# A value pass packed into 37 columns in place of 54

## Chip, cores, metric

One core of a Trainium2 chip runs the whole program. The metric is the device time of one execution in microseconds (us), lower is better. Engines: PE multiplies matrices (PEld loads its weights), DVE and ACT work on vectors, POOL does general work and issues indirect DMAs, SP issues plain DMAs.

## What is computed

A trunk of two layers for 256 tokens of width 1024. In each layer a token mixer with cross-attention to 256 memory tokens is followed by a layer norm, a PEER feed-forward part and a second norm. The change concerns PEER alone, which has 16384 experts per layer; each token picks 16 for each of 8 heads:

```python
def block(xb):                                   # n = 128 tokens
    q = (xb @ w_q).reshape(n, PEER_HEADS, 2, PEER_HALF)
    s = jnp.einsum('nhpc,pkc->nhpk', q, sk)      # two keys, 128 values each
    sv, si = lax.top_k(s, 16)
    cand = sv[:, :, 0, :, None] + sv[:, :, 1, None, :]
    cand_id = si[:, :, 0, :, None] * 128 + si[:, :, 1, None, :]
    fv, fi = lax.top_k(cand.reshape(n, PEER_HEADS, 256), 16)
    eid = cand_id at fi                          # expert numbers
    gw = jax.nn.softmax(fv, axis=-1)
    act = gelu(jnp.einsum('nhkd,nd->nhk', u_tab[eid], xb))
    return jnp.einsum('nhk,nhkd->nd', gw * act, v_tab[eid])
```

The inputs are drawn with large query, key and expert weights, so that the softmax is steep.

## The kernel before

The program is traced once, so that loops in the code are instructions in a row. Every weight block passes through one machine. `plan` (L1330 on) writes a list `items` in the order of use. `load` (L142) brings an item into one of 5 buffers `raw`: a plain item with a DMA on SP (L150), an item that is a number with an indirect gather on POOL (L156), whose row numbers lie in `vrow`. `pump` (L102) splits an item exactly into a high part `wH` (ACT, L122) and a rest `wL` (DVE, L137, or POOL, L132 and L135); each has 3 buffers. `mm3` (L194) makes three products from the parts, L196 to L198.

PEER does not gather experts by token. It computes dense: expert number = first key × 128 + second key, and the 128 experts with one second key form a column, which is one block of 128 × 1024. Coefficients lie in `lo` (tile `wglo`) for the 64 columns with second key under 64 and in `hi` (`wghi`) for the other 64, by expert and token. The scatter (L1236) puts the routing weight, scaled by 32768 and stored as two fp16 numbers, in its place; the Gelu of the expert's product multiplies it (`finish`, `gated`). Most entries stay 0.

The value pass is the loop `for i in range(NC)` in `peer_layer`. Its first 64 steps, the plain columns, take `lo` and the value table in order. The next `COLS` steps, the packed columns, take only those of the 8192 experts of `hi` that have a coefficient other than 0. `coef(i)` splits the coefficients of column i two steps ahead (`cH` on ACT L251, `cL` on DVE L252), `next` pumps the value blocks three ahead, and `products` makes for each half of the tokens (128) and each half of the width one `mm3` of 128x512: 6 products for one token half, 12 for both. After the last columns, which are kept (3 in layer 0, 6 in layer 1), come the norm and the next stage.

The list of used experts is made on the way by the generator `lists`, one piece per column. It marks for each expert of `hi` which token half uses it, and orders them: only the first half, both, only the second. In that order they get consecutive places in the packed columns. So the first half needs columns 0 to `A_END` − 1, the second columns `B_BEG` to `COLS` − 1 (`blocks`, and `column_order`, which mixes columns of one half with those of both). This holds if the counts fit, which three tests find out; `go` is 1 if all hold:

```python
ok[:, 0:1] = sc[:, nj - 1:nj] >= float(P * B_BEG)          # only the first half
ok[:, 1:2] = sc[:, 2 * nj - 1:2 * nj] <= float(P * A_END)  # first half
ok[:, 2:3] = sc[:, 3 * nj - 1:3 * nj] <= float(P * COLS)   # all
ids = ids * ok                                             # 0 if one fails
```

(shortened from L1080 to L1111). With `crow`, made from `ids`, `lists` gathers the coefficients of each packed column from `rows`, a copy of `hi` in DRAM, two columns per step (`FIRST_GATHER`; `wghi<-rows`, POOL L156). Row 0 of `rows` is zero and stands for an empty place. Afterwards the same queue gathers the values by `vrow` (`raw<-in_v_dram,words`).

Then `dense` (L1123 on) reads `go` on PE and SP and tests it (L1127). If it is 0, the branch loads all 64 value blocks of `hi` and their coefficients into the tile `words` (SP, L1131 and L1132) and makes four products for each in full precision (L255, two instructions each); the packed columns then carry zeros and run all the same. All engines pass the branch.

In layer 0, the items of the next layer's cross-attention, four of `memT` (512 wide) and four of `wkv` (1024 wide), are put between the packed columns (the memory parts). Each takes a `raw` buffer, a cast and a subtraction, but no product in the pass.

Of the kernel before, what the change touches and what calls it, by code (L numbers as in the profile page):

```python
# [25 lines left out]
N0 = 64  # L26
# [2 lines left out]
RAW_BUFS, HL_BUFS = 5, 3  # L29
POOL_COLS = 512  # L30
HALF_COLS = 384
COLS, A_END, B_BEG = 54, 40, 13
NC = N0 + COLS
BIG = 127.0 * 128.0
FIRST_GATHER = 2
STEP_US = 2.65
LATE = 3
EXTRA = 3
# [28 lines left out]
class Trunk:  # L67
# [938 lines left out]
    def lists(self, layer, hi):  # L1006
# [109 lines left out]
        order = self.order[layer]  # L1116
        for k in range(0, COLS, FIRST_GATHER):
            for c in order[k:k + FIRST_GATHER]:
                self.gather(hi[:, c, :], self.rows, crow[:, c:c + 1])
# [17 lines left out]
    def peer_layer(self, layer):  # L1137
        nc, tc, A = self.nc, self.tc, self.A
        with ExitStack() as ctx:
# [11 lines left out]
            with ExitStack() as rctx:  # L1151
# [16 lines left out]
                def route():  # L1168
                    for tt in range(2):
                        for q in range(2):  # L1170
                            self.score(qT, sk, ss[tt], tt, q)
                            yield STEP_US
                    self.pool_cols = D
                    for tt in range(2):
                        yield from self.keys16(w, tt, ss[tt], range(4))
                    while not self.asked:
                        yield STEP_US
                    for tt in range(2):
                        for q in range(2, 4):
                            self.score(qT, sk, ss[tt], tt, q)  # L1180
                        yield STEP_US
                    for tt in range(2):
# [9 lines left out]
                    for _ in range(LATE):  # L1192
                        yield STEP_US
                    self.ready()

                def paced():
                    budget = 0.0
                    for c in route():
                        budget -= c
                        while budget <= 0:  # L1200
                            yield
                            budget += STEP_US - (0.2 + (D - self.pool_cols) / 960 if self.pool_cols < D else 0)
                self.asked = False
# [126 lines left out]
    def plan(self):  # L1330
        A = self.A

        def w(name, n, dts=range(DT)):
            for dt in dts:
                self.add(A[name][dt], n)

        def part(name, dst, k, pool=True):
            fl = lambda t: t[:, 2 * k:2 * k + 2, :].rearrange("p a b -> p (a b)")
            to = lambda: (fl(dst()[0]), fl(dst()[1]))
            to.pool = pool  # L1340
            self.add(A[name][k], 512, to)

        def first(name):
            w(name, 1024, range(3))
            for k in range(4):
                part("memT", lambda: self.mem, k)
                w(name, 1024, (3 + k,))
            w(name, 1024, (7,))

        def norm(n, layer):  # L1350
            for k in "gb":
                ap = A[f"{n}_{k}"][layer]
                self.add(bass.AP(tensor=ap.tensor, offset=ap.offset, ap=[[0, P], [1, D]]), D, None, k)

        def tail(layer):
            for i, dt in enumerate((6, 7, 0, 1, 2, 3, 4, 5)):
                self.add(A["w_out"][layer, dt], D, i - 2 if 0 <= i - 2 < EXTRA else None)
            norm("ln1", layer)
            for g in range(2):
                for dt in range(DT):  # L1360
                    self.add(A["w_q"][layer, g, dt], D)
            for i in range(P):
                self.add(A["u"][layer, i], D)
            for i in range(NC):
                e = i - NC + HL_BUFS + EXTRA
                self.add(A["v"][layer, i] if i < N0 else self.order[layer][i - N0], D,
                         e if layer and 0 <= e < EXTRA else None)
                k = (i - N0 - 4) // 6
                if layer == 0 and i > N0 and (i - N0 - 4) % 6 == 0 and 0 <= k < 8:
                    if k < 4:  # L1370
                        part("memT", lambda: self.mem, k, False)
                    else:
                        self.add(A["wkv"][1, k - 4], D, lambda c=k - 4: self.kvw[c])
            norm("ln2", layer)
        for dt in range(DT):
            self.add(A["xT"][dt // 2][:, dt % 2 * T:(dt % 2 + 1) * T], T,
                     lambda dt=dt: (self.xH[:, dt, :], self.xL[:, dt, :]))
            self.add(A["w0kg"][dt], 896, cuts=2 if dt < 2 else 1)
        first("w0qx")
        for c in range(4):  # L1380
            self.add(A["wkv"][0, c], D)
        w("w0v", 768)
        w("w0o", 768)
        tail(0)
        w("w1x", 1024)
        w("w1g", 768)
        tail(1)

    def build(self):
# [85 lines left out]
```

## Time and profile before

| | |
|---|---|
| median of 3 runs | 2051.15 us (2051.14 to 2054.2) |
| profiled execution, its own time | 2052.67 us |
| its span, first to last instruction | 2050.9 us |
| mean granted PE clock | 0.987 |
| PE, DVE, ACT, POOL busy | 95%, 66%, 44%, 34% |
| moved by DMA | 396.69 MB |

The profile is of one execution. A group of instructions is named by line, engine, operation and tiles (out<-in); its columns are busy time and mean time of one, then the engine's idle time just ahead of them and what ended it. A product is pipelined: its time (0.39 us) is longer than the distance to the next one, which is what counts. A DMA's landing time is from issue to the last byte.

### The profile page before, as it was taken

The page shows a single profiled execution, that of the slowest core. Times are in us where ns is not written, and L with a number is a line of the kernel's source. Part 1 is how long each engine was busy: PE and PEld are TensorE (multiplying, and loading weights), DVE is VectorE, ACT ScalarE, POOL GpSimd, SP SyncE. Part 2 cuts the span into 40 slices and gives each one's busy share as a digit, 9 for nine tenths or more (in the row PEclk, how much of TensorE's full clock was granted, in tenths as well). Part 3 has the DMA queues.
Part 4 walks back from the last instruction along what each step waited for, and adds up shares of the span by engine and source line. Part 5 has one row for each costly group of instructions (what it writes and reads, how often), then busy time and mean ns, then how long its engine had stood idle before and what let it go on. Part 6 is the DMA issues. An engine that isn't in the chain of part 4 may idle for free.

```text
span 2050.9 us, 34035 instructions
## 1 busy us (share of the span) xinstructions
PE 1952.3 (95%) x12909; PEld 1670.1 (81%) x12909; DVE 1355.4 (66%) x2779; ACT 907.6 (44%) x1566; POOL 688.8 (34%) x553
## 2 busy tenths in 40 slices
PE   8999999999999998998899999999999768999997
PEld 8999999999987776788799999999878543333586
DVE  5674877799999755777848768999997320000276
ACT  5455455555454445646355555554544220000264
POOL 2026832433310376522368334333103450000263
PEclk9999999999999999999999999999999989999999
DMA  6555566556577688765255665566776994555475
GB/s 229 175 174 189 177 194 196 176 165 200 181 220 243 210 249 231 268 240 167 71 185 180 195 195 176 159 203 187 221 240 177 166 228 165 168 172 172 153 265 174
DMA packets 149289, 396.69 MB, mean 193 GB/s; under 512 B 14589, under 2 KB 58626, under 8 KB 148866
## 3 DMA queue, kind: packets, MB, share of 16 engines
q1 hardware_dynamic: 93464, 303.76, 46.4%
q0 software_dynamic: 20736, 70.79, 12.8%
q10 hardware_dynamic: 34922, 19.93, 3.2%
q8 instruction: 102, 1.67, 0.3%
q14 instruction: 65, 0.53, 0.1%
HBM read 376.59 MB, written 17.83 MB: 192 GB/s over the span
## 4 chain that ended last, share of the span: by engine, by line
PE 54%; issue 17%; DMA 13%; POOL 8%; ACT 3%; DVE 3%; SPq 1%; POOLq 0%; DVEq 0%; ACTq 0%
PE bank L197 15%; PE bank L198 15%; PE bank L196 15%; PE bank L255 8%; POOL wL L132 6%; DMA words<-rows 6%; DMA raw<-in_v_dram,words 3%; DMA raw<-in_v_dram 2%; ACT wH L122 1%; POOL raw L156 1%; DVE wL L137 1%; DMA raw<-in_w0kg_dram 1%; SPq L1131 0%; POOL wghi L156 0%; POOL wL L135 0%
## 5 line engine op out<-in xcount | busy, mean ns | idle before, releaser
L122 ACT CAST wH<-raw 128x1024 fp32r<-128x1024 f32 (+2 forms) x584 | 606.1, 1039 | 1024.6 <-PE bank L198 475.0
L137 DVE TENSOR_TENSOR wL<-raw,wH 128x1024 fp32r<-128x1024 f32 (+3 forms) x387 | 437.1, 1133 | 608.7 <-ACT wH L122 606.0
L196 PE MATMUL bank<-xHL,wH 128*128 128x256 f32 x2536 | 715.0, 282 | 0.6 <-ACT wH L122 0.5
L198 PE MATMUL bank<-xHL,wL 128*128 128x256 f32 x2536 | 702.8, 277 | 5.0 <-DVE wL L137 4.8
L197 PE MATMUL bank<-xHL,wH 128*128 128x256 f32 x2536 | 702.2, 277 | 2.2 <-DVE xHL L252 2.1
L198 PEld LDWEIGHTS bank<-xHL,wL 128*128 128x128 f32 x2536 | 476.4, 188 | 7.0 <-DVE wL L137 6.8
L197 PEld LDWEIGHTS bank<-xHL,wH 128*128 128x128 f32 x2536 | 477.0, 188 | 3.0 <-DVE xHL L252 3.0
L196 PEld LDWEIGHTS bank<-xHL,wH 128*128 128x128 f32 x2536 | 476.6, 188 | 1.3 <-ACT wH L122 1.2
L196 PE MATMUL bank<-wH,cH 128*128 128x512 f32 x827 | 328.9, 398 | 21.0 <-ACT cH L251 14.9
L135 POOL TENSOR_TENSOR wL<-raw,wH 128x1024 fp32r<-128x1024 f32 (+1 forms) x124 | 265.0, 2140 | 222.7 <-ACT wH L122 221.9
L197 PE MATMUL bank<-wL,cH 128*128 128x512 f32 x827 | 328.6, 397 | 11.5 <-DVE wL L137 11.4
L198 PE MATMUL bank<-wH,cL 128*128 128x512 f32 x827 | 326.7, 395 | 0.0
L255 PE MATMUL bank<-words 128*128 128x512 f32 x512 | 233.0, 607 | 33.3 <-DMA words<-rows 33.3
L156 POOL DMA_INDIRECT raw<-in_v_dram,words x108 | 133.8, 1239 | 343.5 <-DVE wL L137 270.0
L255 PEld LDWEIGHTS bank<-words 128*128 128x128 f32 x512 | 94.6, 192 | 171.2 <-issue 96.7
L132 POOL TENSOR_TENSOR wL<-raw,wH 128x386 fp32r<-128x386 f32 x126 | 129.6, 1029 | 279.9 <-DVE wL L130 279.9
L156 POOL DMA_INDIRECT wghi<-rows,words x108 | 114.5, 1060 | 272.6 <-DVE words L1113 226.1
L196 PEld LDWEIGHTS bank<-wH,cH 128*128 128x128 f32 x827 | 157.2, 190 | 59.9 <-ACT cH L251 20.8
L197 PEld LDWEIGHTS bank<-wL,cH 128*128 128x128 f32 x827 | 157.4, 190 | 52.8 <-DVE wL L137 21.1
L198 PEld LDWEIGHTS bank<-wH,cL 128*128 128x128 f32 x827 | 157.6, 191 | 34.4 <-DVE cL L252 0.3
L962 DVE TENSOR_TENSOR oh<-iota,i12T 128x1024 f16<-128x1024 f16 x128 | 130.3, 1018 | 0.0
L130 DVE TENSOR_TENSOR wL<-raw,wH 128x640 fp32r<-128x640 f32 x126 | 103.9, 824 | 7.8 <-ACT wH L122 0.3
(330 smaller groups left out, 1885.1 us busy)
## 6 DMA issues: line engine op xcount, KB each, us to landing
raw<-in_u_dram SPq DMA_DIRECT2D x256, 512.0 KB, 3.5
raw<-in_v_dram SPq DMA_DIRECT2D x128, 512.0 KB, 4.2
words<-in_v_dram SPq DMA_DIRECT2D x64, 512.0 KB, 3.5
raw<-in_w_q_dram SPq DMA_DIRECT2D x32, 512.0 KB, 3.8
rows<-wghi ACTq DMA_DIRECT2D x32, 512.0 KB, 5.0
raw<-in_w_out_dram SPq DMA_DIRECT2D x16, 512.0 KB, 4.0
words<-rows SPq DMA_DIRECT2D x64, 128.0 KB, 3.5
raw<-in_w0qx_dram SPq DMA_DIRECT2D x8, 512.0 KB, 5.0
```

The source lines that it names most:

```text
L122: (nc.vector.tensor_copy if self.cast_dve else nc.scalar.copy)(h[:, c], r[:, c])
L130: nc.vector.tensor_sub(l[:, k:], r[:, k:], h[:, k:].bitcast(F32))
L132: nc.gpsimd.tensor_sub(l[:, :k], r[:, :k], h[:, :k].bitcast(F32))
L135: nc.gpsimd.tensor_sub(l[:, :k], r[:, :k], h[:, :k].bitcast(F32))
L137: nc.vector.tensor_sub(l[:, k:], r[:, k:], h[:, k:].bitcast(F32))
L156: self.nc.gpsimd.indirect_dma_start(out=dst, out_offset=None, in_=table, in_offset=bass.IndirectOffsetOnAxis(ap=rows, axis=0))
L196: mm(out, sH, mH, start=start, stop=False, skip_group_check=True)
L197: mm(out, sH, mL, start=False, stop=False, skip_group_check=True)
L198: mm(out, sL, mH, start=False, stop=stop, skip_group_check=True)
L255: self.nc.tensor.matmul(out, lhsT, rhs, start=start, stop=stop, skip_group_check=True)
L962: nc.vector.tensor_tensor(flat(oh[:, 1:3]), self.iota2.unsqueeze(1).to_broadcast([P, 4, P, 2]), pairs(self.i12T[:, j]), op=ALU.is_equal)
```

## The change

```diff
-COLS, A_END, B_BEG = 54, 40, 13
+COLS, A_END, B_BEG = 37, 23, 11
 NC = N0 + COLS
 BIG = 127.0 * 128.0
 FIRST_GATHER = 2
+MEM_STEP = 4
...
-                k = (i - N0 - 4) // 6
-                if layer == 0 and i > N0 and (i - N0 - 4) % 6 == 0 and 0 <= k < 8:
+                k = (i - N0 - 3) // MEM_STEP
+                if layer == 0 and i > N0 and (i - N0 - 3) % MEM_STEP == 0 and 0 <= k < 8:
```

There are 37 packed columns in each layer in place of 54. Columns 0 to 10 are for the first token half alone (before: 0 to 12), 11 to 22 for both (13 to 39), 23 to 36 for the second alone (40 to 53). The three tests compare with 11, 23 and 37 times 128. The memory parts come after packed columns 3, 7 and so on to 31 (before: 4, 10 and so on to 46). Behind the new line, line numbers are higher by 1.

On POOL the row gathers of layer 0 stand like this before (`wghi` are coefficients, `raw` value blocks; the branch row is the test of `go`):

```order
L156 DMA wghi_4672<-rows_75,words_7907 128x256 x38
L156 DMA raw_9357<-in_v_dram,words_7907 128x1024
L156 DMA wghi_4672<-rows_75,words_7907 128x256 x2
L156 DMA raw_9381<-in_v_dram,words_7907 128x1024
...
L156 DMA raw_9547<-in_v_dram,words_7907 128x1024
L1127 UNCONDITIONAL_BRANCH
...
L156 DMA raw_9571<-in_v_dram,words_7907 128x1024
L156 DMA raw_9983<-in_v_dram,words_7907 128x1024
```

and with the change:

```order
L157 DMA wghi_4672<-rows_75,words_7907 128x256 x37
L1128 UNCONDITIONAL_BRANCH
L157 DMA raw_9356<-in_v_dram,words_7907 128x1024
L157 DMA raw_9774<-in_v_dram,words_7907 128x1024
L157 DMA raw_9796<-in_v_dram,words_7907 128x1024
L157 DMA raw_9818<-in_v_dram,words_7907 128x1024
L157 DMA raw_9862<-in_v_dram,words_7907 128x1024
L522 MEMSET kmT_9871 128x1024
L523 MEMSET vm_9872 128x1024
L157 DMA raw_9906<-in_v_dram,words_7907 128x1024
```

All coefficient gathers and the branch now stand ahead of the first value gather; before, the last 16 were mixed with the value gathers.

On DVE, at the first packed columns of layer 0, before (`cL` 128x128 is a column of one token half, 128x256 of both; `memL` is a memory part):

```order
L252 TENSOR_TENSOR cL_9502<-wghi_4672,cH_9501 128x256
L137 TENSOR_TENSOR wL_9520<-raw_9381,wH_9519 128x1024
L252 TENSOR_TENSOR cL_9526<-wghi_4672,cH_9525 128x128
L137 TENSOR_TENSOR wL_9544<-raw_9405,wH_9543 128x1024
L252 TENSOR_TENSOR cL_9550<-wghi_4672,cH_9549 128x256
L1127 UNCONDITIONAL_BRANCH
L137 TENSOR_TENSOR wL_9568<-raw_9429,wH_9567 128x1024
L252 TENSOR_TENSOR cL_9574<-wghi_4672,cH_9573 128x128
L137 TENSOR_TENSOR wL_9980<-raw_9453,wH_9979 128x1024
L252 TENSOR_TENSOR cL_9986<-wghi_4672,cH_9985 128x256
L137 TENSOR_TENSOR memL_9491<-raw_9477,memH_9490 128x512
```

and with the change:

```order
L253 TENSOR_TENSOR cL_9887<-wghi_4672,cH_9886 128x256
L138 TENSOR_TENSOR wL_9903<-raw_9774,wH_9902 128x1024
L253 TENSOR_TENSOR cL_9909<-wghi_4672,cH_9908 128x128
L138 TENSOR_TENSOR wL_9925<-raw_9796,wH_9924 128x1024
L253 TENSOR_TENSOR cL_9931<-wghi_4672,cH_9930 128x128
L138 TENSOR_TENSOR wL_9947<-raw_9818,wH_9946 128x1024
L253 TENSOR_TENSOR cL_9953<-wghi_4672,cH_9952 128x256
L138 TENSOR_TENSOR memL_9876<-raw_9840,memH_9875 128x512
```

Columns of one half and of both alternated; now two or three of one half follow each other, and the first memory part comes one column earlier. The branch has moved seven plain columns ahead of them.

## Prediction

> **What bounds the kernel now.** The page first: its span and its slices of busy tenths for PE and DVE.
>
> ```profile
> span 2050.9 us, 34035 instructions
> ...
> PE   8999999999999998998899999999999768999997
> ...
> DVE  5674877799999755777848768999997320000276
> ```
>
> PE is busy nearly everywhere, so time is won by removing PE work or PE waits. Slices 34 to 37 have a busy PE and an idle DVE, which no other part has. The program's name for what runs there is the tile `words`; its view:
>
> ```profile
> L255 PE MATMUL bank<-words x512: 591/592/1222, 1662.4 to 1928.1; 128*128 128x512 f32 x171
> ...
> L156 POOL DMA_INDIRECT wghi<-rows,words x108: 943/949/1948, 697.8 to 1678.8; - x108
> ...
> L1131 SPq DMA_DIRECT2D words<-in_v_dram x64: 327/328/1084, 1640.1 to 1921.0; - x64
> ```
>
> The 64 loads of line 1131 are one pass through the branch of `dense`, and all lie in layer 1. So layer 1's flag `go` was 0 and the 54 packed columns did not hold its experts; layer 0's flag was 1. I then cut the two value passes into stretches (columns: bounds, length, then busy time and count of PE, PEld, DVE, ACT, POOL, the granted clock, DMA share, GB/s).
>
> ```profile
> 583.71:764.53 180.82, 178.74 (x836) 146.71 (x835) 145.11 (x211) 87.04 (x129) 52.91 (x54) 1.00 0.75 237
> 764.53:901.02 136.49, 121.42 (x489) 92.58 (x488) 87.75 (x121) 75.64 (x116) 73.00 (x62) 0.96 0.79 247
> 1453.58:1659.66 206.08, 188.74 (x837) 149.36 (x836) 144.52 (x210) 86.93 (x129) 51.99 (x54) 0.98 0.80 210
> ...
> 1662.38:1928.17 265.79, 232.47 (x513) 94.44 (x512) 2.98 (x4) 2.60 (x4) 13.15 (x13) 0.97 0.58 170
> 1928.17:2043.25 115.08, 112.01 (x494) 90.69 (x492) 80.13 (x114) 67.45 (x103) 61.95 (x49) 0.99 0.62 219
> ...
> 1935.00:2015.00 80.00, 80.00 (x355) 66.26 (x354) 59.40 (x83) 53.01 (x83) 53.86 (x41) 1.00 0.74 262
> 800.00:890.00 90.00, 84.71 (x357) 65.74 (x356) 65.25 (x87) 56.26 (x86) 47.80 (x39) 1.00 0.79 272
> ```
>
> In order: layer 0's 64 plain columns, its packed columns; layer 1's plain columns, the branch, its packed columns (one more ran at 1659.66, 2.7 us); two stretches inside the packed parts. Layer 1's plain columns do the same work as layer 0's and take 25.3 us longer. A full PE does 355 products in 80 us, 0.225 us each.
>
> **The branch: which test failed, and will it fail again?** The old tests are: only the first token half needs at least 13 columns, the first half at most 40, all at most 54. I counted the reference's own routing (experts with second key from 64, in columns of 128; only first, first half, all). Every chosen expert counted: layer 0 14.6, 38.6, 52.4; layer 1 14.2, 37.3, 51.2. Both would pass, against the rows. But the weight times 32768 is kept in fp16, where anything below 2^-25 becomes 0, and the softmax is steep. Without those: layer 0 13.8, 21.6, 34.6; layer 1 12.7, 20.0, 33.5. Now layer 0 passes and layer 1 fails on 12.7 under 13, as the rows say. If the Gelu zeroes some more, all counts fall; layer 0's first must stay at 13 or above, and there layer 1's is about 12.0. The new limits are 11, 23, 37: both layers pass, by at least 1.0, 1.4 and 2.4 columns. So the branch goes: −265.8 us.
>
> **The slow plain columns of layer 1.** With `go` 0 every index is 0, so all gathers of line 156 read one row. Landing times, layer 0 from 697 to 750, then layer 1 from 1590 to 1640:
>
> ```profile
> raw<-in_v_dram SPq DMA_DIRECT2D x18, 512.0 KB, 4.1
> wghi<-rows,words POOLq DMA_INDIRECT x38, 4.7
> ```
> ```profile
> raw<-in_v_dram SPq DMA_DIRECT2D x10, 512.0 KB, 24.7
> wghi<-rows,words POOLq DMA_INDIRECT x23, 14.7
> ```
>
> Same instructions, 14.7 us for 4.7, and the loads beside them 24.7 for 4.1. With distinct rows I take layer 0's stretch for layer 1: −25.3 us.
>
> **The packed columns.** A column read by one half costs 6 products, by both 12. Before, 27 + 2×27 = 81 blocks, 486 products, 109 us; now 25 + 2×12 = 49, 294 products, 66.2 us; 43 us of PE go per layer. PE takes them only as fast as its supply comes, and columns now average 7.9 products (1.79 us) instead of 9 (2.03 us). The supply, by groups from 800 to 890 us, with the median landing of those gathers:
>
> ```profile
> L137 DVE TENSOR_TENSOR wL<-raw,wH 128x1024 fp32r<-128x1024 f32 x41 | 49.9, 1222 | 25.4 <-ACT wH L122 25.3
> L156 POOL DMA_INDIRECT raw<-in_v_dram,words x39 | 48.0, 1231 | 37.9 <-DVE cL L252 16.5 <-DVE wL L137 12.3 <-issue 4.6
> ...
> L122 ACT CAST wH<-raw 128x1024 fp32r<-128x1024 f32 x41 | 43.1, 1051 | 32.8 <-DMA raw<-in_v_dram,words 21.4 <-PE bank L198 6.1 <-DVE cL L252 2.9
> ...
> L252 DVE TENSOR_TENSOR cL<-wghi,cH 128x128 fp32r<-128x128 f32 (+1 forms) x40 | 13.8, 346 | 0.0
> ...
> L137 DVE TENSOR_TENSOR kL<-raw,kH 128x1024 fp32r<-128x1024 f32 x4 | 5.0, 1260 | 0.0
> L122 ACT CAST kH<-raw 128x1024 fp32r<-128x1024 f32 x4 | 4.2, 1043 | 0.0
> L137 DVE TENSOR_TENSOR memL<-raw,memH 128x512 fp32r<-128x512 f32 x2 | 1.4, 688 | 0.1
> ```
> ```profile
> raw<-in_v_dram,words POOLq DMA_INDIRECT x39, 6.1
> ```
>
> It is a ring: a gather waits for one of 5 `raw` buffers, which DVE frees (releasers L252, L137), then ACT waits for the gather. One turn is 0.3 of issue + 6.1 + 1.05 + 1.22 = 8.7 us; over 5 buffers 1.73 us an item. Measured, with PE a bound for part of the stretch, 41 + 4 + 2 items in 90 us, 1.91. I take 1.8, since PE's share of that bound goes. [...]
>
> Layer 0 has 37 columns and 8 memory parts, the latter now after every 4th column instead of every 6th, each taking a turn: 45 items. When PE reaches the first, 8 are under way (5 raw, 3 split); 37 turns remain, 66.6 us. The tail from the last gather's issue, and the branch test's stall:
>
> ```profile
> 697.83 1.15 POOL L156 DMA_INDIRECT wghi<-rows,words  x1 [113.03 <-DVE words L1113]
> 750.38 1.16 POOL L156 DMA_INDIRECT raw<-in_v_dram,words  x1 [0.30 <-DMA raw<-in_v_dram]
> 770.36 0.97 POOL L521 MEMSET kmT<- 128x1024 f32 x1
> 884.40 1.03 POOL L156 DMA_INDIRECT raw<-in_v_dram,words  x1 [0.30 <-issue]
> 2019.27 0.94 POOL L156 DMA_INDIRECT raw<-in_v_dram,words  x1 [0.30 <-issue]
> ```
> ```profile
> 769.63 0.47 PE L196 MATMUL bank<-wH,cH 128*128 128x512 f32 x1 [2.22 <-PEq L1127]
> ...
> 772.30 0.63 PE L198 MATMUL bank<-wH,cL 128*128 128x512 f32 x1
> 772.73 0.63 PE L196 MATMUL bank<-wH,cH 128*128 128x512 f32 x1
> ```
>
> Tail: 884.40 to 901.02, 16.6 us. The test now stands ahead of plain column 57, so seven plain columns queue behind it on PE, but it costs the same: 2.2 us, and about eight products at 0.43 us (772.30 to 772.73) in place of 0.225, 3.9 us together. Layer 0: 66.6 + 16.6 + 3.9 = 87.1 for 136.5, −49.4 us. Layer 1 has no parts: 37 − 8 = 29 turns, 52.2, plus 2019.27 to 2043.25, 24.0, plus 3.9: 80.1 for 115.1 + 2.7, −37.7 us.
>
> **Small and free edits.** Line 1091's 64 products per layer shrink from 108 to 74 columns: 34/512 × 0.225 × 64 = 1.0 us each layer, −1.9. POOL has 37 row gathers instead of 54; now none stands between the value gathers, which before were issued every third (before: 697.83 to 750.38 for 38, 1.38 us each; after: done at about 749). They still start in time: 749 is 15 us ahead of PE's 764.53. POOL's two fills, 0.97 us each, move behind the fifth value gather; that lead hides them, else they cost 1.9. SP's queue has its own test:
>
> ```profile
> SPq L1127 <- SPq L1127: 3.3, 1, 3.3
> ```
>
> All 64 plain loads stand before it; the first memory part, which stood before it too, now stands behind. It is 3.3 us late at most and has three columns (5 us) ahead of it; uncovered, 3.3. DVE in layer 0's packed part needs 37 × (1.22 + 0.35) + 4 × 1.26 + 4 × 0.69 = 66 us, hidden by the ring's 45 × 1.8 = 81; without that cover it would bind like PE's 66. The last memory part follows column 31, so all are there before their use after column 36.
>
> **Sum.** 49.4 + 25.3 + 265.8 + 37.7 + 1.9 = 380.1; the span falls from 2050.9 to 1670.8. The profiled execution took 2052.67, 1.77 around its span; the median is 1.5 below it. Forecast 1671.
>
> **The rivals.**
> *PE keeps up with the supply.* If transfers land faster than 6.1 us, PE bounds both layers: 66.2 + 3.9 = 70.1 each, gains 66.4 and 47.7; 407 in all, 1644; with a few us of last waits 1650. Layer 1's full stretch of 80 us speaks for it, ACT's 21.4 us of waits for gathers against.
> *The clock falls in the hungry columns.* Layer 1 shows it:
>
> ```profile
> 1609.58 0.50 PE L196 MATMUL bank<-wH,cH 128*128 128x512 f32 x1 [1.47 <-ACT cH L251]
> ...
> 1612.41 0.63 PE L198 MATMUL bank<-wH,cL 128*128 128x512 f32 x1
> ...
> 1610.00:1620.00 10.00, 7.79 (x24) 5.30 (x23) 2.38 (x4) 1.78 (x3) 6.04 (x6) 0.83 0.94 158
> ```
>
> A gap of 1.47 us was followed by products at half pace and 0.83 mean clock. That hides behind the supply except in the tails (3 and 6 columns, 36 and 72 products): at half pace +8 and +16 us at most; I put this at 1685. [...]
> *Layer 0 or 1 still takes the branch.* If one list overflows: +265.8 + 25.3 × 37/54 = 283: 1954.
> *Slower: both take it.* One mechanism: the tables are cut below what the lists hold. It decides when the first half needs over 2944 experts (23 × 128) or all over 4736 in both layers. Then 1671 + 566 = 2237. My count stands 1.4 and 2.4 columns off; a count with every chosen expert would be far over, but the branch rows exclude it.
>
> **How the numbers follow.** Forecast 0.74, clock 0.11, PE-bound 0.08, one branch 0.04, two 0.03. Ring at 1.73 gives gains 4.6 more (2.6 + 2.0), at 1.91 7.3 less (4.1 + 3.2): 1666 to 1678; the range reaches to the two near rivals, 1650 to 1690. A measurement tells 0.2% (4 us). Faster 0.97, same 0, slower 0.03.
>
> **What would show it.** Right: no product of line 255's kind (now 256) anywhere; layer 1's plain columns near 181 us with row gathers landing near 5 us; packed stretches of about 83 and 76 us with ACT waiting for gathers, PE under nine tenths. Wrong: 256-line products in either layer (the count), packed stretches near 67 us with no gather waits (the ring), or a clock near 0.8 in the last columns.

## The result, and the profile after

| | before | after |
|---|---|---|
| median, same chip | 2052.13 us (4 runs, 2051.14 to 2054.2) | 1683.09 us (4 runs, 1681.01 to 1688.04) |
| ratio, 95% interval | | 0.8204 [0.8184, 0.8224] |
| profiled execution, span | 2052.67, 2050.9 us | 1682.1, 1680.3 us |

The change takes 369 us off, 18%. The forecast was 1671 (1650 to 1690), 12 us too low. The page of after, span and busy slices:

```profile
span 1680.3 us, 31641 instructions
...
PE   9999999999999999999798899999999999999896
...
DVE  5675586949999999757668846697699999996476
```

The four slices with a busy PE and an idle DVE are gone. The view of the tile `words` has no product of line 256 and no load of line 1132:

```profile
L157 POOL DMA_INDIRECT wghi<-rows,words x74: 942/1104/1994, 693.2 to 1566.1; - x74
L157 POOL DMA_INDIRECT raw<-in_v_dram,words x74: 935/945/1989, 744.6 to 1647.5; - x74
```

37 gathers of each kind per layer, and no branch in either. The stretches, cut as in the prediction: plain and packed columns of layer 0, of layer 1; then one steady piece of each packed part (columns as there: length, PE, PEld, DVE, ACT, POOL, clock, DMA share, GB/s).

```profile
580.29:762.30 182.01, 178.05 (x837) 145.80 (x835) 142.90 (x211) 87.06 (x129) 47.34 (x49) 1.00 0.74 235
762.30:850.99 88.69, 74.30 (x295) 53.74 (x294) 61.86 (x87) 51.83 (x81) 39.48 (x33) 1.00 0.75 255
1404.12:1591.03 186.91, 180.67 (x836) 147.71 (x835) 143.86 (x211) 87.05 (x129) 46.34 (x48) 0.98 0.73 230
1591.03:1672.70 81.67, 74.95 (x313) 56.86 (x311) 57.51 (x84) 47.26 (x73) 44.34 (x35) 0.96 0.66 223
775.00:835.00 60.00, 49.52 (x192) 34.86 (x192) 42.12 (x59) 36.56 (x58) 30.93 (x26) 1.00 0.80 271
1600.00:1645.00 45.00, 43.04 (x181) 33.04 (x180) 34.80 (x50) 30.70 (x49) 33.17 (x25) 1.00 0.86 290
```

Where the 370.6 us of span went: layer 0's value pass took 317.3 and takes 270.7 (46.6 less); layer 1's, with the branch, took 589.7 (1453.58 to 2043.25) and takes 268.6 (321.1 less). The pass of layer 0 begins 3.4 us earlier (580.29 against 583.71), in code that the change doesn't touch; between and behind the passes 0.5 us are lost.

Layer 1's landing times from 1510 to 1565, where the row gathers of line 157 run:

```profile
raw<-in_v_dram SPq DMA_DIRECT2D x20, 512.0 KB, 4.7
wghi<-rows,words POOLq DMA_INDIRECT x36, 5.0
```

The row gathers land in 5.0 us (14.7 before), the plain loads beside them in 4.7 (24.7). The packed part of layer 0 by groups, 775 to 835 us, and the median landing of its gathers:

```profile
L157 POOL DMA_INDIRECT raw<-in_v_dram,words x26 | 32.1, 1236 | 29.4 <-DVE cL L253 18.4 <-DVE wL L138 8.5 <-issue 1.2
L138 DVE TENSOR_TENSOR wL<-raw,wH 128x1024 fp32r<-128x1024 f32 x26 | 31.8, 1227 | 18.8 <-ACT wH L123 18.6
L123 ACT CAST wH<-raw 128x1024 fp32r<-128x1024 f32 x26 | 27.1, 1048 | 23.4 <-DMA raw<-in_v_dram,words 21.8 <-PE bank L199 1.6
```
```profile
raw<-in_v_dram,words POOLq DMA_INDIRECT x26, 6.0
```

It is the ring again: POOL waits for a buffer that DVE frees, ACT for the gather (21.8 us), DVE for ACT. PE is busy 49.5 of the 60 us. In layer 1's steady piece the ring is less plain: there PE is busy 43.0 of 45 us, so the sign "PE under nine tenths" held in layer 0 only. And the way past the branch on PE's sequencer (L1128; shortest, median and longest time in ns, then first and last start), then the products behind it in each layer:

```profile
L1128 PEldq COMPARE_BRANCH  x2: 5532/6760/7987, 737.5 to 1561.2; - x2
```
```profile
743.15 0.47 PE L197 MATMUL bank<-wH,cH 128*128 128x512 f32 x1 [2.07 <-PEq L1128]
743.46 0.39 PE L198 MATMUL bank<-wL,cH 128*128 128x512 f32 x1
```
```profile
1569.31 0.77 PE L197 MATMUL bank<-wH,cH 128*128 128x512 f32 x1 [4.35 <-PEq L1128]
...
1574.14 0.63 PE L199 MATMUL bank<-wH,cL 128*128 128x512 f32 x1
1574.56 0.53 PE L197 MATMUL bank<-wH,cH 128*128 128x512 f32 x1
```

In layer 0 PE's branch took 5.5 us; PE still had products to work on for all but 2.07 of it, and no product behind it was slow. In layer 1 it took 8.0 us, 4.35 were idle, and twelve products at 0.43 us followed, 2.4 us more.

### The profile page after: what moved, and what is told of

Its sections match the earlier page's. It is cut to its first block, busy times and chain, and to the rows that moved or that the text cites. A ratio compares the mean times of both kernels' runs of the same rounds, so it can differ in the third digit from the quotient of the medians.

```text
span 1680.3 us, 31641 instructions
## 1 busy us (share of the span) xinstructions
PE 1622.9 (97%) x12013; PEld 1498.2 (89%) x12013; DVE 1298.8 (77%) x2711; ACT 861.4 (51%) x1498; POOL 611.3 (36%) x485
## 5 line engine op out<-in xcount | busy, mean ns | idle before, releaser
L123 ACT CAST wH<-raw 128x1024 fp32r<-128x1024 f32 (+3 forms) x550 | 569.9, 1038 | 706.2 <-PE bank L199 213.6
L138 DVE TENSOR_TENSOR wL<-raw,wH 128x1024 fp32r<-128x1024 f32 (+3 forms) x353 | 396.5, 1127 | 296.8 <-ACT wH L123 292.8
L197 PE MATMUL bank<-wH,cH 128*128 128x512 f32 (+1 forms) x699 | 276.2, 395 | 13.2 <-ACT cH L252 6.7
L198 PE MATMUL bank<-wL,cH 128*128 128x512 f32 (+1 forms) x699 | 276.3, 395 | 12.1 <-DVE wL L138 11.9
L199 PE MATMUL bank<-wH,cL 128*128 128x512 f32 (+1 forms) x699 | 274.3, 392 | 0.0
L197 PEld LDWEIGHTS bank<-wH,cH 128*128 128x128 f32 x699 | 132.1, 189 | 43.5 <-ACT cH L252 12.8
L157 POOL DMA_INDIRECT wghi<-rows,words x74 | 79.1, 1068 | 245.6 <-DVE words L1114 223.7
L199 PEld LDWEIGHTS bank<-wH,cL 128*128 128x128 f32 x699 | 132.0, 189 | 28.2 <-DVE cL L253 0.2
L157 POOL DMA_INDIRECT raw<-in_v_dram,words x74 | 91.6, 1238 | 80.5 <-DVE cL L253 41.7
L966 DVE TENSOR_TENSOR oh<-oh,gT 128x1024 f16<-128x1024 f16 x128 | 90.0, 703 | 4.4
L1237 PE MATMUL bank<-oh 128*128 128x128 f16 x1024 | 80.6, 219 | 1.1 <-DVE oh L966 1.1
```

The source lines that it names most:

```text
L123: (nc.vector.tensor_copy if self.cast_dve else nc.scalar.copy)(h[:, c], r[:, c])
L138: nc.vector.tensor_sub(l[:, k:], r[:, k:], h[:, k:].bitcast(F32))
L157: self.nc.gpsimd.indirect_dma_start(out=dst, out_offset=None, in_=table, in_offset=bass.IndirectOffsetOnAxis(ap=rows, axis=0))
L197: mm(out, sH, mH, start=start, stop=False, skip_group_check=True)
L198: mm(out, sH, mL, start=False, stop=False, skip_group_check=True)
L199: mm(out, sL, mH, start=False, stop=stop, skip_group_check=True)
```

## Experiments

The theory to be tested: layer 1 took the branch for the first of the three tests alone; its slow plain columns came from gathers that all read one row; the packed columns are paced by the ring of 5 buffers and its gathers. The rivals: another test failed, so that it was the narrower packing that mattered to the branch; the slow plain columns belong to layer 1 in some other way; PE, the bytes, or POOL's issue sets the pace.

The runs fell on several chips, which differ (before: 2052 us on the chip of the result, 2060 with the first four runs, 2086 and 2081 with two later groups). Times are compared within a group, or as a ratio to before in the same group. Where neither a range nor an interval stands beside a time, the kernel ran once.

### Only the first limit, in the kernel before

```diff
-COLS, A_END, B_BEG = 54, 40, 13
+COLS, A_END, B_BEG = 54, 40, 11
```

> The kernel before with one number changed: the second token half may begin at column 11 in place of 13; still 54 columns, 40 for the first half, memory parts as before. Theory (in layer 1 only the test on the experts of the first half alone failed, 12.7 columns under 13): the branch in layer 1 is gone (-265.8 us) and so are the slow plain columns (-25.3); two more columns are for both halves, 12 products of 0.225 us more per layer (+5.4): 1765 us, no L255 products, plain columns of layer 1 near 182 us. Rival (one of the other two tests failed, so that the gain came from the count of columns): the branch stays, 2051 to 2056 us.

Measured 1778.24 us, before there 2060.32 (0.863). Layer 1's plain and packed columns:

```profile
1455.53:1636.40 180.87, 178.79 (x836) 146.70 (x835) 145.02 (x211) 87.04 (x129) 52.93 (x54) 1.00 0.76 236
1636.40:1768.53 132.13, 120.67 (x517) 96.87 (x515) 83.45 (x118) 70.31 (x107) 78.34 (x64) 0.95 0.72 225
```

No branch, and the plain columns at 180.9 where before had 206.1: the 25.3 us of the prediction to a tenth (layer 0 of this run: 180.8). So one number out of three brings 282 of the 369 us, and the first test alone had failed. One thing was not foreseen: without the branch the 54 packed columns take 132.1 us, not 115.1 + 2.7, which is 14.3 us more. Two more columns for both halves are 2.7 us of that, 12 products at 0.225. PE is also idle for 8.4 us more: 11.5 us of the 132.1, against 3.1 of the 115.1. The test here stands at the first packed columns, where the branch on PE took 5.9 us from 1635.5 us on; in the kernel before, the 31.8 us behind the branch have PE busy throughout. The mean clock is 0.95 against 0.99. What the other 3 us are is not shown.

### The first limit put back, in the changed kernel

```diff
-COLS, A_END, B_BEG = 37, 23, 11
+COLS, A_END, B_BEG = 37, 23, 13
```

> The changed kernel with the second half beginning at column 13 again: 37 columns, 23 for the first half. Theory: layer 1 fails on the first test once more (12.7 under 13) and takes the branch, layer 0 (13.8) does not: 1683 + 265.8 + 17 for the one-row gathers - 5 for two columns of one half in place of both, about 1961 us. Rival: no branch in either layer, 1678 us; or both layers take it, about 2240 us.

Measured 1968.69 us, in the same group. The view of `words`:

```profile
L256 PE MATMUL bank<-words x512: 592/592/1193, 1605.6 to 1858.0; 128*128 128x512 f32 x171
```

The branch is back, in layer 1 alone: one pass of 512 instructions, 253 us. Layer 0 fills at least 13 columns with experts of the first half only, layer 1 fewer than 13. Layer 0 of this run, with the test and with row gathers of spread rows, is the measure for two runs of the same group below; its plain columns:

```profile
581.58:765.30 183.72, 179.66 (x837) 146.94 (x835) 142.88 (x211) 87.04 (x129) 47.32 (x49) 0.99 0.75 233
```

### Limits drawn closer: 35, 22, 12

```diff
-COLS, A_END, B_BEG = 37, 23, 11
+COLS, A_END, B_BEG = 35, 22, 12
```

> The changed kernel with limits just outside the counts: 35 columns, 22 for the first half, the second from 12 (counted: layer 0 34.6, 21.6, 13.8; layer 1 33.5, 20.0, 12.7). Theory (the counts are right): no branch; 45 blocks in place of 49, 5.4 us of PE work per layer, but the supply sets the pace: two turns of 1.9 us fewer per layer, -7.6: 0.816 of before, 7 to 8 us under the changed kernel. Rival (the counts are off by more than half a column): one layer takes the branch, +280 us. Second rival (PE sets the pace): -11 us.

Measured 1979.2 us (1972.69 to 1993.66), ratio 0.9493 [0.944, 0.9547]. The view of `words`:

```profile
L256 PE MATMUL bank<-words x512: 592/592/1193, 1618.4 to 1871.2; 128*128 128x512 f32 x171
```

A miss: the branch in layer 1. With 12 it fails and with 11 it holds, if it is the first test that failed here; the prediction's count for layer 1 was 12.7, and 12.0 if the Gelu zeroes more. So fewer experts are in use there than were counted. The margin of the change itself is therefore under one column in layer 1 (128 experts), not "at least 1.0".

### Limits from the corrected counts: 33, 20, 11

```diff
-COLS, A_END, B_BEG = 37, 23, 11
+COLS, A_END, B_BEG = 33, 20, 11
```

> 33 packed columns, the first half of the tokens in 20, the second in 22 (limits 33, 20, 11). Corrected theory of the counts: layer 1's first-only experts fill between 11 and 12 columns (the run with limits 35, 22, 12 branched in layer 1, the one with 11 did not), layer 0's between 13 and 13.3; of the cut-offs of small weights that give both, every one leaves the first half at most 19.8 columns and all at most 32.6, so no test fails and no branch runs. Ring theory: four columns fewer at 1.9 us in each layer, 15 us less than the control, 0.813 of the time before; packed parts 81 and 74 us. Rival, PE sets the pace: 7 blocks of 6 products at 0.225 us fewer in each layer, 19 us less. Rival, the counts are off again: the branch in one layer, 270 to 285 us more.

The changed kernel went along unchanged, as a control:

> The changed kernel again, as a control on the same chip as the next two. Expected 0.820 of the time before (1683 us where the kernel before takes 2052).

Measured, in the group with before at 2081.18: control 1719.93 us, 0.8262 [0.8238, 0.8286]; 33 columns 1704.45, 0.8187 [0.8167, 0.8208]. No branch. That settles that it was the first test which failed with 35, 22, 12: with 33 and 20 the other two limits are lower still, and they hold. It also shows the prediction's counts for these two too high: all experts in use fit 33 columns in both layers (counted 34.6 and 33.5), and layer 0's of the first half fit 20 (counted 21.6). So the margins of the change there are wider than was said, and that of the first test is narrower; which small coefficients become 0 was not measured. Control, then 33 columns, packed parts of layers 0 and 1:

```profile
786.00:871.10 85.10, 74.50 (x296) 53.68 (x295) 61.83 (x87) 52.20 (x82) 39.73 (x33) 1.00 0.80 266
...
1629.25:1710.80 81.55, 74.05 (x313) 56.23 (x311) 57.13 (x84) 47.09 (x73) 43.62 (x35) 0.98 0.66 225
```
```profile
783.97:862.60 78.63, 65.57 (x254) 46.80 (x253) 56.10 (x79) 46.99 (x74) 36.77 (x30) 0.98 0.79 262
...
1618.22:1694.60 76.38, 67.46 (x271) 49.01 (x269) 51.62 (x77) 41.84 (x65) 37.69 (x31) 0.93 0.63 211
```

The 15.5 us less are what was expected, but the packed parts give 6.5 + 5.2 = 11.7 of them and not 15: layer 1's ran at a clock of 0.93. The rest lies in the plain columns (2.6 and 0.3 less) and between the passes, and isn't explained.

### The changed kernel without the test

```diff
-        self.dense(layer, go, words[:, 512:], self.y)
```

It leaves out the branch for lists that overflow, which these inputs do not take.

> The changed kernel without the branch and its test (the way out for lists that do not fit is left out). Theory: the test costs its PE gaps, 2.07 us in layer 0 and 4.35 in layer 1, and about 2.5 us of half-pace products behind the second: 9 us, 1674 us; layer 1's plain columns fall from 187 to about 180 us. Rival: value gathers are held anyway and another wait takes its place, 1681 to 1684 us.

Measured 1674.16 us (1673.97 to 1674.19), 0.8124 [0.811, 0.8138]. All four stretches:

```profile
581.56:761.23 179.67, 177.78 (x836) 145.85 (x835) 142.88 (x211) 87.05 (x129) 47.33 (x49) 1.00 0.76 238
761.23:848.90 87.67, 75.13 (x296) 55.17 (x295) 61.49 (x87) 51.81 (x82) 41.45 (x33) 0.98 0.79 259
1403.59:1583.28 179.69, 177.81 (x837) 145.85 (x835) 143.35 (x211) 87.05 (x129) 46.29 (x48) 1.00 0.77 239
1583.28:1664.80 81.52, 75.24 (x313) 57.19 (x311) 57.23 (x84) 47.01 (x73) 41.64 (x35) 0.96 0.66 224
```

Plain columns of 179.7 us in both layers, against 182.0 and 186.9 with the test: by that it costs 2.3 and 7.2 us, and layer 1's plain columns are otherwise just like layer 0's. The packed parts change by 1.0 and 0.2, so they do not hold the test's cost. The two kernels ran on different chips; the ratios differ by 0.0080, 16 us, more than these 9.5. On this run's chip layer 0 with limit 13 put back has 183.7, so there the test costs 4.0 us.

### All row gathers read one row

```diff
-        nc.vector.tensor_copy(crow, ids)
+        nc.vector.tensor_scalar(crow, ids, 0.0, None, op0=ALU.mult)
```

`crow` is 0 throughout, `vrow` and `go` are as before; the packed columns get coefficients of zero.

> The changed kernel, with all gathers of coefficients reading row 0 in both layers (the packed coefficients are left out, zeros take their place); no branch is taken. Theory (one row for all is what made the gathers slow): row gathers land in about 15 us in place of 5, and the plain columns of both layers grow by 25.3 x 37/54 = 17 us: 1717 us. Rival (layer 1's slow columns before had another cause, such as the clock or the coming branch): gathers land near 5 us, 1683 us.

Measured 1735.64 us. The plain columns, then the landing times from 700 to 770 us, then the branch on PE:

```profile
582.67:791.85 209.18, 188.54 (x837) 150.00 (x835) 142.93 (x211) 87.00 (x129) 45.08 (x49) 0.95 0.78 204
...
1433.85:1645.08 211.23, 188.90 (x837) 150.28 (x836) 143.26 (x211) 86.98 (x129) 45.16 (x48) 0.94 0.79 203
```
```profile
raw<-in_v_dram SPq DMA_DIRECT2D x16, 512.0 KB, 21.4
wghi<-rows,words POOLq DMA_INDIRECT x35, 15.4
```
```profile
L1128 PEldq COMPARE_BRANCH  x2: 11272/12170/13067, 759.0 to 1610.3; - x2
```
With nothing changed but which rows are read, both layers get the slow gathers (15.4 us, plain loads 21.4) and slow plain columns: 25.5 us more in layer 0 than with limit 13 put back, in the same group, and 27 and 24 over the changed kernel's on the other chip. That is the second theory shown, and it holds for layer 0 as for layer 1. It is more than the 17 us expected; the branch on PE, which now takes 11.3 and 13.1 us in place of 5.5 and 8.0, makes up part of that.

One thing limits the finding. With `go` 0 the value gathers of the kernel before have one index for all rows too (`vrow` is made from `ids`). In its layer 1, from 1935 to 2015 us, 41 of them landed in 5.8 us, no later than layer 0's 6.1 from spread rows. So it is the row gathers, 128 KB from `rows`, that one row makes slow, and not the value gathers, 512 KB from the value table. Why they differ is open.

### What sets the pace of the packed columns

Three kernels on one chip (before there 2086.16 us). The changed kernel as the control:

> The changed kernel itself, beside the next three on one chip: 1683 us, or 0.820 of the kernel before.

The packed value blocks by plain loads of SP, from layer 0's table in order (not the values of the used experts, but the same bytes and the same buffers):

```diff
-                self.gather(r, self.A["v"].rearrange("l i p d -> (l i p) d"), self.vrow[:, ap:ap + 1])
+                self.nc.sync.dma_start(r, self.A["v"][0, N0 + ap])
```

> The changed kernel with the packed value blocks loaded by plain DMAs on SP, block by block of layer 0's table (the values are not those of the used experts). Same bytes, same 5 buffers. Theory (ring): plain loads landed in 4.1 us, so a turn is 0.1 + 4.1 + 1.05 + 1.22 = 6.5 us, 1.3 an item; packed columns about 75 us in each layer, 17 us less. Rival (bytes): 1.87 us an item as before, no change.

And seven buffers in place of five for the value gathers, two of them in space that is free from plain column 62 on:

```diff
+MORE = 2
...
-        while self.n_load < upto and self.n_flight < RAW_BUFS:
+        while self.n_load < upto and self.n_flight < RAW_BUFS + self.more:
...
-            r = self.raw.tile([P, D], F32, name="raw")[:, :n]
+            self.turn += type(ap) is int
+            own = type(ap) is int and self.more and self.turn % (RAW_BUFS + self.more) < self.more
+            r = (self.raw2 if own else self.raw).tile([P, D], F32, name="raw")[:, :n]
...
+                if i + 2 == N0:
+                    self.raw2 = right.enter_context(tc.tile_pool(name=f"raw2_{layer}", bufs=MORE, side="right"))
+                    self.more = MORE
```

> The changed kernel with two more buffers for value gathers, from column 62 on, in the space that the plain coefficients leave. Theory (the ring of 5 buffers sets the pace of the packed columns): a turn of 8.7 us over 7 buffers is 1.24 us an item, so PE (66 us) or DVE (66 us) becomes the bound, packed columns take about 75 us in each layer in place of 88.7 and 81.7: 18 to 20 us less, 0.811 of before. Rival (bytes set the pace, 512 KB at 280 GB/s are 1.87 us): landing grows from 6 to about 8 us, the time stays within 3 us of the changed kernel. Second rival (DVE's chain sets it): no gain in layer 0, some in layer 1.

Measured: control 1726.78 us (1717.29 to 1730.27), 0.8259 [0.8223, 0.8295]; plain loads 1696.87; seven buffers 1714.76 (1703.41 to 1728.66), 0.8224 [0.8165, 0.8283]. The times alone don't tell the seven buffers from five; the stages do. Packed parts of the control, of seven buffers (with a steady piece of layer 1), and of plain loads (the same):

```profile
788.33:875.30 86.97, 74.05 (x296) 53.83 (x295) 61.85 (x87) 52.14 (x82) 41.01 (x33) 1.00 0.79 261
...
1638.36:1720.00 81.64, 75.56 (x313) 56.48 (x311) 57.66 (x84) 47.17 (x73) 40.79 (x35) 0.96 0.66 224
```
```profile
789.72:871.30 81.58, 73.01 (x296) 55.20 (x295) 61.35 (x87) 51.89 (x82) 39.23 (x33) 0.98 0.78 278
...
1628.60:1702.60 74.00, 70.53 (x313) 55.55 (x311) 56.72 (x84) 46.73 (x73) 41.00 (x35) 1.00 0.71 247
...
1636.00:1678.00 42.00, 41.26 (x180) 33.18 (x179) 34.70 (x51) 31.22 (x51) 32.41 (x27) 1.00 0.93 322
```
```profile
785.69:858.80 73.11, 70.82 (x296) 54.24 (x295) 61.61 (x87) 52.83 (x82) 0.00 (x0) 1.00 0.89 306
...
1614.51:1686.70 72.19, 69.70 (x313) 55.83 (x311) 56.45 (x85) 46.98 (x73) 3.27 (x4) 1.00 0.72 248
...
1630.00:1670.00 40.00, 38.90 (x167) 30.86 (x166) 34.93 (x51) 31.74 (x51) 0.00 (x0) 1.00 0.94 325
```

Two more buffers take 5.4 and 7.6 us off the packed parts, so the ring does set the pace; in layer 1 the mean clock rose with it, from 0.96 to 1.00. It is less than the 18 to 20 us expected: layer 0's part was to come to 75 us and takes 81.6. DVE's chain as the bound is out, by which layer 0 would have gained nothing. In layer 1 it is then no longer the ring. POOL's gathers by group and by waits, 1636 to 1678 us, seven buffers:

```profile
L161 POOL DMA_INDIRECT raw<-in_v_dram,words x27 | 32.9, 1218 | 9.6 <-issue 7.9 <-DVE cL L257 1.7
```

POOL waits 1.7 us for buffers in 42 and issues the rest of the time, 1.22 + 0.3 for a gather, 42 us / 27 = 1.56 each; PE is busy 41.3 of the 42, so the two are full together. With plain loads the same bytes come at 325 GB/s and PE is full (38.9 of 40): bytes do not bind at the changed kernel's 223 to 255. The plain loads take 13.9 and 9.5 us off, where PE as the bound was to give 17.0 and 10.0 (83.2 and 76.2 to 66.2).

### Both: 33 columns and seven buffers

The edits of the two sections above together.

> 33 columns (20 and 22) and the two further buffers for value gathers from plain column 62 on. If the two gains are separate: 5.4 and 7.6 us for the buffers (measured with 37 columns) and four columns at 1.56 us in each layer, 25 us less than the control, 0.808 of the time before. If POOL's issue already binds with seven buffers the columns' part stays 12 us; if PE binds the columns' part is 19 us and the buffers bring nothing more. Branch in a layer: 270 to 285 us more.

Measured 1691.94 us (1683.75 to 1694.83), 0.8126 [0.8095, 0.8158], where the control has 0.8262 and 33 columns alone 0.8187:

```profile
785.76:858.00 72.24, 63.21 (x254) 47.34 (x253) 55.56 (x79) 46.65 (x74) 39.01 (x30) 0.98 0.83 286
...
1612.77:1680.50 67.73, 62.63 (x271) 48.96 (x269) 50.82 (x77) 41.58 (x65) 34.67 (x31) 0.97 0.68 239
```

It is 28 us under the control (25 expected), and the packed parts are 12.9 and 13.8 us shorter: the gains add up. This version beats both kernels.

### A trace of before on another chip

On the two chips with before at 2081 to 2086 us the changed kernel's plain columns took 203 to 210 us, not 182 to 187. In layer 0's plain columns of the control of the ring's group PE's longest gap is 6.70 us, in the middle of the row gathers:

```profile
735.08 0.79 PE L197 MATMUL bank<-wH,cH 128*128 128x512 f32 x1 [6.70 <-ACT wH L123]
```

> The kernel before, unchanged, for a trace of it on whichever chip this is. Two chips gave before 2081 to 2086 us and the changed kernel's plain columns 203 to 210 us in place of 182 to 187. If this chip is such a one (time over 2070 us) and the slow plain columns belong to the chip, before's plain columns of layer 0 take over 195 us too (180.8 in the first trace); if they come from the changed order of the gathers, they stay within 5 us of 181. If the chip is like the first one (about 2052 us), the run tells nothing of this.

Measured 2057.7 us, a chip like the first: plain columns of layer 0 180.8 us. It tells nothing of the others. Whether before is slow there in the same columns stays open; the ratios there, 0.826, are a little above the 0.820 of the result.

## Why the prediction was right, and where it was off

**Branch and slow plain columns: right.** The failing test, the layer, the 25.3 us and their cause are each shown (limits 54, 40, 11; limit 13 put back; one row for all). That gives 282 of the 369 us. All gathers of line 156 did read one row, as the prediction says, but that slowed the row gathers and not the value gathers (5.8 us). "Both layers pass, by at least 1.0, 1.4 and 2.4 columns" was too sure for the first: the true margin in layer 1 is under one column, while the counts behind the other two limits were too high. That a weight below 2^-25 becomes 0 was an assumption of the count; no run shows where the cut-off lies. The rival of one branch, at 0.04, was nearer than it looked: a first limit of 12 for 11 meets it.

**The ring: right in kind, its size 5.5 us short in each layer.** Without the test's share the packed parts were forecast at 83.2 and 76.2 us and took 88.7 and 81.7. The last value gathers were issued here:

```profile
835.60 1.03 POOL L157 DMA_INDIRECT raw<-in_v_dram,words  x1 [0.30 <-issue]
```
```profile
1647.50 1.16 POOL L157 DMA_INDIRECT raw<-in_v_dram,words  x1 [0.31 <-issue]
```

PE's first packed products are at 762.30 and 1591.03 us, so that is 73.3 and 56.5 us. The step that failed is "8 are under way": 6 were in each layer (five value gathers and a memory part in layer 0, six gathers in layer 1), so 39 and 31 turns remained, not 37 and 29; at 1.8 us that is 3.6 of the 5.5 us in each. The seventh item, a gather, followed 0.30 and 0.06 us later; whoever counts it as under way has one turn missing, 1.8 us, and the rest of the 5.5 in a slower pace. The late test is not the cause: without it, 6 are under way too. The plain columns' own turns, one gather for one column that PE finishes, stand at 2.7 us just ahead, so the ring is perhaps not yet as full as its buffers allow; that is argued, not shown:

```profile
1585.65 0.94 POOL L157 DMA_INDIRECT raw<-in_v_dram,words  x1 [0.92 <-DVE wL L138]
1588.37 0.94 POOL L157 DMA_INDIRECT raw<-in_v_dram,words  x1 [1.78 <-DVE wL L138]
```

The turns themselves came at 1.88 and 1.82 us with 6 under way, 1.92 and 1.88 with 7, against the 1.8 that was taken and its 1.73 to 1.91. The tails, 15.4 and 25.2 us for 16.6 and 24.0, cancel.

**The test: put at the wrong place, and one price for two.** It was to cost "the same" as before, 3.9 us in each layer, and this was added to the packed parts. It falls in the plain columns and costs 2.3 and 7.2 (4.0 in layer 0 on the other chip). Before, PE met it after the first 38 row gathers; now it stands among the row gathers in both layers, and in layer 1 the branch took 8.0 us. Together 1.7 us over the forecast. The prediction counted PE's gap (2.2 us) and not the branch's own duration (5.7 us in layer 0 of before).

**The sum.** Layer 0 gained 46.6 for 50.4 with its share of line 1091's products, layer 1 321.1 for 329.8, the start 3.4 for nothing, 0.5 lost between: 370.6 for 380.1. The misses are 11 of ring, 1.7 of test and the 0.5, less the 3.4 of start, 9.8 us where 9.5 are missing.

**The rivals.** PE-bound: refuted, since gathers still land in 6.0 us (775 to 835 us) and PE waits; but with plain loads it is nearly true, and with seven buffers in layer 1 too, where POOL's issue is full as well. The clock: in kind there, in size not. Before the last columns of layer 1 stands a gap of 1.70 us, and ten products at 0.43 us or more follow:

```profile
1654.54 0.79 PE L197 MATMUL bank<-wH,cH 128*128 128x512 f32 x1 [1.70 <-ACT cH L252]
...
1656.51 0.63 PE L197 MATMUL bank<-wH,cH 128*128 128x512 f32 x1
```

From 1660 us on the pace is full again; the ten took 5.5 us where 0.225 each makes 2.3, so some 3 us are lost where the rival had up to 16. The time came out at the rival's 1685 all the same, for another reason. In this the range was lucky: by the ring alone the forecast was 1666 to 1678, which 1683 is outside of, and its upper end stood at 1690 for the clock. The gap of 1.70 us, behind several of 0.2 to 0.7, was followed by slow products and the gap of 2.07 us in layer 0 by none, so here the length of the gap alone did not decide.

## To carry to other kernels

Where a fast path has a test and a slow way out, look first which way each layer takes, and try the failing limit alone: here one number gave three quarters of the gain. A data-dependent limit that is tightened needs its margin measured by a run on each side, not counted from a model of the arithmetic. The ring of five buffers was put at turn time over buffers, 1.73 us an item, and came at 1.82 to 1.92; two more buffers, made from space that had become free, took 5.4 and 7.6 us off the packed parts, until another engine was full (POOL's issue and PE, both in layer 1).

## What the runs showed of the hardware

- **Jumping over the branch's code on PE took 3.7 to 13.1 us.** The compare and branch of PE's sequencer took 0.08 and 0.19 us in two of before's three and 5.7 in the third, the jump of layer 0 among its row gathers. Where it jumped with the last row gather issued 17 us or more ahead, it took 3.7 to 4.0 us (33 columns, and the changed kernel itself on the two chips where PE comes to it later); among row gathers 5.5 and 8.0 in the changed kernel, 6.7 and 5.9 in the kernel before with limit 11; beside one-row gathers 11.3 and 13.1. So in these runs it was longer beside gathers; why is not shown.
- **Row gathers whose indices are all equal took three times as long, and slowed the loads beside them.** They landed in 15.4 us, against 4.8 in the changed kernel, where the rows are spread (128 KB each, from `rows`), and the plain loads beside them in 21.4 against 4.8. The 512 KB value gathers of one row were not slow: 5.8 us.
- **The chips differed in one stage.** The same kernel's plain columns took 182 and 187 us on one chip and 203 to 210 on two others, with all other stages within 4 us. PE's long gaps there lie at the row gathers: in the control of the ring's group 17.5 of layer 0's 19.6 idle us from 705 to 755 us, and 22.4 of layer 1's 24.7 from 1545 to 1595, with the last row gathers issued at 743.4 and 1588.6; why is not shown.
